# Swapped rows in the 2x2 products of a SwiGLU FFN, joined banks in another order, and modulation steps held in a chunk's last pair

## The chip, the cores and the metric

One core of one Trainium2 chip. The metric is the device time of one execution in microseconds; a kernel's time is the median of its runs. The engines are named as in the profile: PE (TensorE, matmuls), DVE (VectorE), ACT (ScalarE), POOL (GpSimd), SP (SyncE, which issues the DMAs here).

## The reference

A trunk of two layers on 640 tokens (128 context, 512 latent) with a width of 1024. Each layer is a SwiGLU FFN, a token mixer of three head groups, and a second FFN; each of the three is modulated by (shift, scale, gate) and closed by a layer norm. The change touches the FFNs alone:

```
def _modulation(cond, w, b):
    return (jax.nn.silu(cond) @ w + b).reshape(cond.shape[0], N_MOD, D_MODEL)

def _ffn_half(x, mod, slot, w1, w3, w2, g, b):
    h = _modulate(x, mod[:, 3 * slot], mod[:, 3 * slot + 1])
    f = (jax.nn.silu(h @ w1) * (h @ w3)) @ w2
    return _residual_post_norm(x, f, mod[:, 3 * slot + 2], FFN_RES, g, b)
```

d_ff is 2816, which is 22 tiles of 128. There are four FFNs in all.

## The kernel before

**Numbers in two parts.** Every matrix operand is held as a high and a low part (hh and hl, wh and wl, gh and gl): a cast on ACT makes the high part, a subtraction the low one. A product takes three matmuls for each step of the contraction: high by high, low by high, high by low. Weights come by DMA into a raw ring of two tiles (wr, L243), are cast by ACT into a ring of six (wh, L299), and the low part wl is a subtraction at L306 on DVE, or on POOL for two of the seven blocks of a pair (s2 and s4). A raw tile is free for the next DMA when its wl is done.

**Chunks.** The 22 tiles of d_ff are taken in chunks of 4, 3, 3, 4, 4 and 4 (ffn, the loop over CHUNKS). The first three tiles of an FFN are made plainly; all others are made by the class Pair: the j-th tile of w1 stands as the top row of a 2x2 block matrix, that of w3 as the bottom row, and the product with the 2x2 blocks of the modulated input (half of the contraction by half, LO and HI, of the 640 columns) is made by seven block products in place of eight. The sums of weight blocks are formed on POOL (L259). Each block product is `prod`: 12 matmuls of 128x320 (L847). The order of the seven on PE is p1, p2, p4, p6, p7, p5, p3.

**What follows a product.** `prod` ends with slot(), which runs the functions that were put off, and then puts off its own; what a function returns runs one slot later. So the work behind a product is emitted behind the next product, and a chain of steps takes one slot each. m is the running sum (pm), g the gate operand (gf), sl the silu operand. C11 = p1+p2 (LO half of the top row), C12 = m+p3 (its HI half), C21 = m-p4 and C22 = m+p5 (the bottom row), with m+p6 and m+p7 on the way. Before, the top row is w1, so silu acts on C11 (c11, L863) and C12 (c12, L877), and g is C21 and C22; gate1 (through L858) and gate2 (L881) multiply, hi (L886) casts gh, lo (L891) makes gl. For the last pair of a chunk the LO half is split on its own (half, L477 and L478) and hi and lo take the HI half; for the other pairs they take all 640 columns.

**The end of a chunk.** After the last pair two tiles of w2 (d0 and d1) are begun with all tiles of the contraction but the last; then the last one is added, half 0 of d0 and d1, half 1 of both (L485), which needs the last pair's gh and gl; tiles d2 to d7 follow, each with its residual on DVE (L610). The weight tiles d0 to d4 are converted ahead, while the last pair runs.

**Banks.** PSUM is held as two joined tiles of two banks (dbl) and four single banks (bank). Before, p4 and p5 share a joined tile; p1, p2, p6, p7 and p3 take single banks. The w2 tiles take joined ones too.

**Modulation on DVE.** In three of the four FFNs part of the next modulation vectors is made on DVE as rows of multiplications with a sum (L460, in the profile scr<-wv,cb; L463 closes one). `mods` adds to a credit at each call and takes as many steps as there is credit. It is called after p2, after p6 and after p5 in every pair, and after each w2 tile.

**The order.** Each engine works through its instructions in the order in which the program emits them; there is no planner.

Of the kernel before, what the change touches and what calls it, by code (L numbers as in the profile page):

```python
# [7 lines left out]
F32 = mybir.dt.float32  # L8
# [10 lines left out]
T = 640  # L19
# [86 lines left out]
def trunk_kernel(tc, I, O):  # L106
# [3 lines left out]
    with ExitStack() as es:  # L110
# [25 lines left out]
        def u(p, n, dt=F32, cols=T, nm="u"):  # L136
            return p.tile([P, cols], dt, tag=nm, name=n)
# [3 lines left out]
        def uid():  # L141
            cnt[0] += 1
            return cnt[0]
# [202 lines left out]
        def start(g):  # L346

            next(g)
            tasks.append(g)
# [480 lines left out]
        class Pair:  # L830


            def __init__(self, h, tb, last):
                self.last = last
                self.b11, self.b21, self.b22 = ([[a[:, c] for a in h[k]] for k in ks]
                                                for ks, c in ((range(4), slice(0, HN)), (range(4, 8), slice(0, HN)),
                                                              (range(4, 8), slice(HN, T))))
                self.t1, self.t2, self.t3, self.t4 = (Quarter(tb, i) for i in range(4))
                self.m, self.sl = u(pe_, f"pm{uid()}"), None

            def out(self):
                self.gh, self.gl = u(pe_, f"gh{uid()}", F32R), u(pe_, f"gl{uid()}", F32R)
                return self.gh, self.gl

            def mms(self, out, w, b, k):
                for i, (a, c) in enumerate(((0, 0), (0, 1), (1, 0))):
                    PE.matmul(out[:, :HN], w[a][:, k, :], b[k][c], start=k == 0 and i == 0, stop=k == 3 and i == 2)  # L847

            def prod(self, out, b, post=None, w=None):
                w = w or ws.get()  # L850
                for k in range(4):
                    self.mms(out, w, b, k)
                slot()
                if post:
                    later.append(post)
# [1 line left out]
            def op(self, o, a, b, f):  # L857
                V.tensor_tensor(out=o, in0=a, in1=b[:, :HN], op=f)  # L858

            def c11(self, p2):  # L860
                self.sl = u(pe_, f"sl{uid()}")
                self.op(self.sl[:, LO], self.m[:, LO], p2, ALU.add)
                return lambda: S.activation(self.sl[:, LO], self.sl[:, LO], AF.Silu) and None  # L863

            def gate1(self):
                self.op(self.g[:, LO], self.g[:, LO], self.sl, ALU.mult)
                return self.half if self.last else None

            def half(self):
                split(self.gh[:, LO], self.gl[:, LO], self.g[:, LO])  # L870

            def c12(self, p3):
                self.op(self.sl[:, HI], self.m[:, LO], p3, ALU.add)
                return self.silu2

            def silu2(self):
                S.activation(self.sl[:, HI], self.sl[:, HI], AF.Silu)  # L877
                return self.gate2

            def gate2(self):  # L880
                V.tensor_tensor(out=self.g[:, HI], in0=self.g[:, HI], in1=self.sl[:, HI], op=ALU.mult)  # L881
                return self.hi

            def hi(self):
                c = HI if self.last else slice(0, T)
                S.copy(self.gh[:, c], self.g[:, c])  # L886
                return self.lo

            def lo(self):
                c = HI if self.last else slice(0, T)  # L890
                V.tensor_tensor(out=self.gl[:, c], in0=self.g[:, c], in1=self.gh[:, c].bitcast(F32), op=ALU.subtract)  # L891

            def start(self):
                p1, p2 = bank("p1"), bank("p2")
                self.prod(p1, self.b11, lambda: S.copy(self.m[:, LO], p1[:, :HN]) and None)
                self.prod(p2, self.b21, lambda: self.c11(p2))

            def run(self, mods, begun=False):
                m, op = self.m, self.op
                if not begun:  # L900
                    self.start()
                mods(0)
                p45 = dbl("p4")
                p4, p5 = p45[:, 0, :], p45[:, 1, :]
                self.prod(p4, self.t4)
                p6 = bank("p6")
                self.prod(p6, self.t2, lambda: op(m[:, LO], m[:, LO], p6, ALU.add))
                mods(1)
                p7 = bank("p7")

                def u3():
                    op(m[:, HI], m[:, LO], p7, ALU.add)
                    self.g = u(pe_, f"gf{uid()}")
                    op(self.g[:, LO], m[:, HI], p4, ALU.subtract)
                    return self.gate1
                self.prod(p7, self.t3, u3)

                def u4():
                    op(self.g[:, HI], m[:, HI], p5, ALU.add)
                    op(m[:, LO], m[:, LO], p5, ALU.add)  # L920
                self.prod(p5, self.t1, u4)
                mods(2)
                p3 = bank("p3")
                self.prod(p3, self.b22, lambda: self.c12(p3))

            def run_first(self, mods, other, ts):

                m, op = self.m, self.op
                self.start()
                mods(0)  # L930
                other.start()
                p3 = bank("p3")
                self.prod(p3, self.b22, None, ws.get(4))
                w22 = ws.get(0)
                p45, p6, p7 = dbl("p4"), bank("p6"), bank("p7")
                p4, p5 = p45[:, 0, :], p45[:, 1, :]
                wq = [ws.get(0), ws.get(0), ws.get(2), w22]
                for k in range(4):
                    for o, w, b in zip((p5, p7, p6, p4), wq, (self.t1, self.t3, self.t2, self.t4)):
                        self.mms(o, w, b, k)  # L940
                    mods(k)
                    next(ts, 0)
                slot()

                def post():
                    self.g = u(pe_, f"gf{uid()}")
                    op(m[:, LO], m[:, LO], p6, ALU.add)
                    op(m[:, HI], m[:, LO], p7, ALU.add)
                    op(self.g[:, LO], m[:, HI], p4, ALU.subtract)
                    op(self.g[:, HI], m[:, HI], p5, ALU.add)  # L950
                    op(m[:, LO], m[:, LO], p5, ALU.add)
                    later.append(self.gate1)
                    return self.c12(p3)
                later.append(post)

        LO, HI = slice(0, HN), slice(HN, T)

# [58 lines left out]
        def ffn(l, f, h, first, nmod, nvec, norm, scale_x, tb, ts):  # L1016
# [5 lines left out]
            ws.convert(ws.n + 2)  # L1022
            ws.lows()

            def mods(when=None):
                if vec[0]:
                    credit[0] += (4 * nvec + 4) / 95 * (1 if when is None else 1)
                    while credit[0] >= 1:
                        credit[0] -= 1
                        next(vec[0], None)  # L1030
                if when is not None and when != 1 and not (f == 0 and ci == 0):
                    return
                if n_left[0]:
# [978 lines left out]
        for l in range(DEPTH):  # L2012
            for f in range(2):
                for j0, j1 in CHUNKS:
                    for j in range(j0, j1):
                        tw = [I["w13"][l, f, j, :, wi] for wi in range(2)]
                        if j < NC:
                            for wi in range(2):
                                ws.tile(tw[wi], (KD, P), "m" if 2 * j + wi == NOPEN else None)
                            continue  # L2020
                        r = ws.pair(*tw)
                        for nm in BLOCKS:
                            ws.block(nm, r)
# [176 lines left out]
```

## Time and profile before

| | |
|---|---|
| Median of three runs | 2698.13 us |
| Lowest and highest | 2695.59, 2703.82 us |
| The profiled execution | 2705.26 us |
| Its span | 2703.3 us |
| PE busy | 2555.0 us, 95% |
| DVE busy | 2072.3 us, 77% |
| ACT busy | 1175.9 us, 43% |
| POOL busy | 1244.0 us, 46% |
| PE waiting for DVE L858 (banks) | 16.8 us, 8 times |
| PE waiting for ACT L886 (gh) | 11.7 us, 13 times |

The span is what the profiler saw of the one execution that was profiled. Shares are of that span. A wait is an engine's idle time before an instruction, put down to the releaser that came last. Busy time of DVE, ACT and POOL counts for the end only where PE waits for it.

### The profile page before, as it was taken

How to read it: one execution, taken by the hardware profiler on the slowest of the kernel's cores; microseconds unless marked ns; L12 is line 12 of the kernel's file. 1: busy time of each engine (PE TensorE's matmuls, PEld its weight loads, DVE VectorE, ACT ScalarE, POOL GpSimd, SP SyncE). 2: the span in 40 equal slices, each digit the busy share in tenths (PEclk: the TensorE clock that was granted, in tenths of full speed). 3: DMA queues.
4: the chain of work that ended last, by engine and by line, in shares of the span. 5: the costliest groups of instructions: out<-in, count | busy, mean ns of one | idle time of the engine just before them, and what ended most of it. 6: DMA issues, size and time to landing. Idle time of an engine off the chain costs nothing. (4 is left out here: it accounts for less than half of the span.)

```text
span 2703.3 us, 49877 instructions
## 1 busy us (share of the span) xinstructions
PE 2555.0 (95%) x18662; PEld 2453.0 (91%) x18662; DVE 2072.3 (77%) x3759; ACT 1175.9 (43%) x2596; POOL 1244.0 (46%) x973
## 2 busy tenths in 40 slices
PE   7999999899999999999989999998998999999997
PEld 6999999888778999999989999998887798999997
DVE  6599889856764879988987998898476558777776
ACT  5233333545575533333353333334545745334333
POOL 2345445522444554544555454454233456435545
PEclk9999999999999999999989999998999999999998
DMA  7333332354344223333222333323543331222222
GB/s 273 116 98 101 111 97 83 117 152 136 91 130 156 71 96 100 103 101 109 68 83 84 112 103 101 110 87 108 158 134 98 103 114 40 82 82 87 79 86 71
DMA packets 130545, 285.89 MB, mean 106 GB/s; under 512 B 16832, under 2 KB 34560, under 8 KB 129664
## 3 DMA queue, kind: packets, MB, share of 16 engines
q1 hardware_dynamic: 130304, 282.70, 33.2%
q8 instruction: 148, 2.42, 0.4%
q14 instruction: 93, 0.76, 0.1%
HBM read 254.95 MB, written 8.81 MB: 98 GB/s over the span
## 5 line engine op out<-in xcount | busy, mean ns | idle before, releaser
L306 DVE TENSOR_TENSOR wl<-wr,wh 128x512 fp32r<-128x512 f32 (+1 forms) x524 | 518.3, 1003 | 74.1 <-ACT wh L299 72.5
L299 ACT CAST wh<-wr 128x512 fp32r<-128x512 f32 (+1 forms) x570 | 333.3, 607 | 479.4 <-DMA wr<-in_w 296.9
L485 PE MATMUL o<-gh,wh 128*128 128x256 f32 (+1 forms) x1408 | 439.5, 312 | 19.4 <-ACT gh L886 11.7
L485 PE MATMUL o<-gl,wh 128*128 128x256 f32 (+1 forms) x1408 | 439.0, 312 | 1.8 <-DVE gl L478 0.3
L485 PE MATMUL o<-gh,wl 128*128 128x256 f32 (+1 forms) x1408 | 436.7, 310 | 0.0
L847 PE MATMUL p<-hh,wh 128*128 128x320 f32 x1216 | 378.4, 311 | 16.8 <-DVE pm L858 16.8
L847 PE MATMUL p<-hl,wh 128*128 128x320 f32 x1216 | 378.2, 311 | 6.2 <-DVE hl L1010 6.2
L847 PE MATMUL p<-hh,wl 128*128 128x320 f32 x1216 | 378.1, 311 | 0.0
L259 POOL TENSOR_TENSOR ws<-wr 128x512 f32<-128x512 f32 x76 | 111.5, 1468 | 545.8 <-DMA wr<-in_w 482.8
L299 ACT CAST wh<-ws 128x512 fp32r<-128x512 f32 x304 | 185.9, 621 | 361.6 <-PE p L847 153.4
L306 POOL TENSOR_TENSOR wl<-ws,wh 128x512 fp32r<-128x512 f32 x152 | 241.3, 1591 | 193.6 <-ACT wh L299 193.1
L610 DVE SCALAR_TENSOR_TENSOR x<-o,gat,x 128x128 f32<-128x128 f32 (+2 forms) x404 | 192.9, 524 | 139.6 <-PE o L485 136.6
L485 PEld LDWEIGHTS o<-gh,wh 128*128 128x128 f32 x1408 | 267.8, 190 | 23.0 <-ACT gh L886 14.5
L485 PEld LDWEIGHTS o<-gl,wh 128*128 128x128 f32 x1408 | 268.1, 190 | 6.7 <-DVE gl L891 4.8
L485 PEld LDWEIGHTS o<-gh,wl 128*128 128x128 f32 x1408 | 267.9, 190 | 0.0
L847 PEld LDWEIGHTS p<-hh,wh 128*128 128x128 f32 x1216 | 229.9, 189 | 19.0 <-issue 18.9
L847 PEld LDWEIGHTS p<-hl,wh 128*128 128x128 f32 x1216 | 230.0, 189 | 7.4 <-DVE hl L1010 7.4
L847 PEld LDWEIGHTS p<-hh,wl 128*128 128x128 f32 x1216 | 230.0, 189 | 0.3 <-DVE wl L306 0.3
L460 DVE SCALAR_TENSOR_TENSOR scr<-wv,cb 128x512 f32<-128x512 f32 x192 | 181.2, 944 | 0.0
L259 POOL TENSOR_TENSOR ws<-wr,wr 128x512 f32<-128x512 f32 x76 | 130.2, 1713 | 0.0
L259 POOL TENSOR_TENSOR ws<-wr,ws 128x512 f32<-128x512 f32 x76 | 129.9, 1709 | 0.0
L259 POOL TENSOR_TENSOR ws<-ws,wr 128x512 f32<-128x512 f32 x76 | 119.1, 1567 | 6.0
(434 smaller groups left out, 6633.9 us busy)
## 6 DMA issues: line engine op xcount, KB each, us to landing
wr<-in_w SPq DMA_DIRECT2D x176, 512.0 KB, 4.2
wm<-in_wmod SPq DMA_DIRECT2D x192, 256.0 KB, 3.9
wr<-in_w SPq DMA_DIRECT2D x128, 256.0 KB, 2.7
wv<-in_wmt SPq DMA_DIRECT2D x96, 256.0 KB, 4.0
wr<-in_w SPq DMA_DIRECT2D x64, 192.0 KB, 2.4
wr<-in_wint SPq DMA_DIRECT2D x24, 512.0 KB, 4.2
wr<-in_wo SPq DMA_DIRECT2D x16, 512.0 KB, 3.8
xd<-x SPq DMA_DIRECT2D x16, 320.0 KB, 5.1
```

Of the source, the lines that this page charges most:

```text
L259: G.tensor_tensor(out=o, in0=x0, in1=x1, op=op)
L299: S.copy(hl[0], src[:, c0:c1])
L306: eng.tensor_tensor(out=t2, in0=src, in1=t.bitcast(F32), op=ALU.subtract)
L460: V.scalar_tensor_tensor(out=scr, in0=w[2 * i + hf], scalar=1.0, in1=cb[:, 2 * st + hf, :], op0=ALU.mult, op1=ALU.mult, accum_out=a[:, 2 * ...
L485: PE.matmul(out[:, :cn], whl[a][:, k, :], b[:, c0:c0 + cn], start=k == 0 and i == 0, stop=k == n - 1 and i == 2)
L610: V.scalar_tensor_tensor(out=c, in0=src, scalar=gat[:, d, s:s + 1], in1=c, op0=ALU.mult, op1=ALU.add)
L847: PE.matmul(out[:, :HN], w[a][:, k, :], b[k][c], start=k == 0 and i == 0, stop=k == 3 and i == 2)
```

## The change

Three things are changed, and the number of instructions stays the same on each engine.

1. **The rows are swapped.** The pair is built as (w3, w1) in place of (w1, w3). The top row is now w3 and the bottom row w1. So silu acts on C21 and C22 (from p4, p5, p6, p7), and the gate operand g is C11 and C12 (from p2 and p3). After p3 there stand: the addition into g, gate HI, gh, gl. The steps move between slots accordingly: silu LO in the slot after p3, gate LO, silu HI, c12 and gate HI in the slot after the next p1, the cast of gh after the next p2, gl after the next p4.
2. **The banks.** p6 and p7 now share a joined tile, as p4 and p5 do. p1, p2 and p3 take single banks.
3. **Modulation.** In the last pair of a chunk the calls of mods after p6 and after p5 add to the credit and take no step; the credit is spent in the calls that follow.

The rest of the diff drops functions that nothing calls.

```
-            def gate1(self):
-                self.op(self.g[:, LO], self.g[:, LO], self.sl, ALU.mult)
-                return self.half if self.last else None
...
+            def gate(self, c):
+                V.tensor_tensor(out=self.g[:, c], in0=self.g[:, c], in1=self.sl[:, c], op=ALU.mult)
+
+            def split(self, c):
+
                 S.copy(self.gh[:, c], self.g[:, c])
-                return self.lo
...
+                def lo():
+                    V.tensor_tensor(out=self.gl[:, c], in0=self.g[:, c], in1=self.gh[:, c].bitcast(F32), op=ALU.subtract)
+                return lo
+
+            def run(self, mods):
+                m, op = self.m, self.op
                 p1, p2 = bank("p1"), bank("p2")
...
+                def c11():
+                    self.g = u(pe_, f"gf{uid()}")
+                    op(self.g[:, LO], m[:, LO], p2, ALU.add)
+                self.prod(p1, self.b11, lambda: S.copy(m[:, LO], p1[:, :HN]) and None)
+                self.prod(p2, self.b21, c11)
                 mods(0)
-                p45 = dbl("p4")
-                p4, p5 = p45[:, 0, :], p45[:, 1, :]
+                p67, p45 = dbl("p6"), dbl("p4")
+                p4, p5, p6, p7 = (p[:, i, :] for p in (p45, p67) for i in range(2))
                 self.prod(p4, self.t4)
-                p6 = bank("p6")
                 self.prod(p6, self.t2, lambda: op(m[:, LO], m[:, LO], p6, ALU.add))
-                mods(1)
-                p7 = bank("p7")
...
+                mods(1, self.last)
+
+                def c21():
+                    self.sl = u(pe_, f"sl{uid()}")
                     op(m[:, HI], m[:, LO], p7, ALU.add)
...
+                    op(self.sl[:, LO], m[:, HI], p4, ALU.subtract)
+
+                    def silu():
+                        S.activation(self.sl[:, LO], self.sl[:, LO], AF.Silu)
+                        return gate1
+                    return silu
+
+                def gate1():
+                    self.gate(LO)
+                    return (lambda: self.split(LO)) if self.last else None
+                self.prod(p7, self.t3, c21)
+
+                def c22():
+                    op(self.sl[:, HI], m[:, HI], p5, ALU.add)
+                    op(m[:, LO], m[:, LO], p5, ALU.add)
+                    return lambda: S.activation(self.sl[:, HI], self.sl[:, HI], AF.Silu) and None
+                self.prod(p5, self.t1, c22)
+                mods(2, self.last)
                 p3 = bank("p3")
...
+                def c12():
+                    op(self.g[:, HI], m[:, LO], p3, ALU.add)
+                    self.gate(HI)
+                    return lambda: self.split(HI if self.last else slice(0, T))
+                self.prod(p3, self.b22, c12)
...
-            def mods(when=None):
+            def mods(when=None, hold=False):
                 if vec[0]:
                     credit[0] += (4 * nvec + 4) / 95 * (1 if when is None else 1)
-                    while credit[0] >= 1:
+                    while credit[0] >= 1 and not hold:
                         credit[0] -= 1
                         next(vec[0], None)
...
-                        r = ws.pair(*tw)
+                        r = ws.pair(*tw[::-1])
```

DVE in the last pair of the fourth chunk, second FFN of layer 0, before: wl_13730 and wl_13752 are the low parts of w2's d0 and d1, gl_13531 that of the pair before, wl_13773 that of d2.

```order
L460 SCALAR_TENSOR_TENSOR scr_11797,va_13723<-wv_13301,cb_11114 128x512
L881 TENSOR_TENSOR gf_13659<-gf_13659,sl_13590 128x320
L858 TENSOR_TENSOR sl_13745<-pm_13682,p_13686 128x320
L306 TENSOR_TENSOR wl_13730<-wr_13639,wh_13729 128x512
L306 TENSOR_TENSOR wl_13752<-wr_13641,wh_13751 128x512
L891 TENSOR_TENSOR gl_13531<-gf_13659,gh_13530 128x640
L858 TENSOR_TENSOR pm_13682<-pm_13682,p_13747 128x320
L306 TENSOR_TENSOR wl_13773<-wr_13749,wh_13772 128x512
```

DVE at the same place after: wl_13704 and wl_13725 are d0 and d1, gl_13502 is the pair before's, wl_13743 is d2.

```order
L865 TENSOR_TENSOR gl_13502<-gf_13565,gh_13501 128x640
L855 TENSOR_TENSOR gf_13719<-pm_13652,p_13656 128x320
L306 TENSOR_TENSOR wl_13704<-wr_13609,wh_13703 128x512
L306 TENSOR_TENSOR wl_13725<-wr_13611,wh_13724 128x512
L855 TENSOR_TENSOR pm_13652<-pm_13652,p_13700 128x320
L306 TENSOR_TENSOR wl_13743<-wr_13722,wh_13742 128x512
```

The low part of the pair before moved from behind the two wl's to ahead of both.

ACT in the same last pair before: wh_13772, wh_13792 and wh_13815 are the casts of d2, d3 and d4; sl_13745, gh_13683 belong to the last pair, sl_13590 and gh_13530 to the one before.

```order
L877 ACTIVATE sl_13590<-sl_13590 128x320
L895 COPY pm_13682<-p_13685 128x320
L299 CAST wh_13729<-wr_13639 128x512
L299 CAST wh_13751<-wr_13641 128x512
L886 CAST gh_13530<-gf_13659 128x640
L863 ACTIVATE sl_13745<-sl_13745 128x320
L299 CAST wh_13772<-wr_13749 128x512
L299 CAST wh_13792<-wr_13770 128x512
L299 CAST wh_13815<-wr_13790 128x512
L477 CAST gh_13683<-gf_13808 128x320
L877 ACTIVATE sl_13745<-sl_13745 128x320
L886 CAST gh_13683<-gf_13808 128x320
```

ACT at the same place after: wh_13742, wh_13761 and wh_13783 are d2, d3 and d4; sl_13776 and gh_13653 belong to the last pair, sl_13628 and gh_13501 to the one before; wh_13678 is the block s4.

```order
L902 ACTIVATE sl_13628<-sl_13628 128x320
L299 CAST wh_13678<-ws_13604 128x512
L862 CAST gh_13501<-gf_13565 128x640
L875 COPY pm_13652<-p_13655 128x320
L299 CAST wh_13703<-wr_13609 128x512
L299 CAST wh_13724<-wr_13611 128x512
L299 CAST wh_13742<-wr_13722 128x512
L299 CAST wh_13761<-wr_13740 128x512
L299 CAST wh_13783<-wr_13759 128x512
L890 ACTIVATE sl_13776<-sl_13776 128x320
L902 ACTIVATE sl_13776<-sl_13776 128x320
L862 CAST gh_13653<-gf_13719 128x320 x2
```

Both silus of the last pair now stand behind the cast of d4; before, the first stood ahead of d2's. The cast of s4 stands behind the second silu of the pair before.

DVE from the last products to the residuals, before:

```order
L460 SCALAR_TENSOR_TENSOR scr_11797,va_13723<-wv_13301,cb_11114 128x512
L306 TENSOR_TENSOR wl_13793<-wr_13770,wh_13792 128x512
L858 TENSOR_TENSOR gf_13808<-gf_13808,sl_13745 128x320
L858 TENSOR_TENSOR gf_13808<-pm_13682,p_13727 128x320
L858 TENSOR_TENSOR pm_13682<-pm_13682,p_13727 128x320
L478 TENSOR_TENSOR gl_13684<-gf_13808,gh_13683 128x320
L858 TENSOR_TENSOR sl_13745<-pm_13682,p_13811 128x320
L881 TENSOR_TENSOR gf_13808<-gf_13808,sl_13745 128x320
L891 TENSOR_TENSOR gl_13684<-gf_13808,gh_13683 128x320
L306 TENSOR_TENSOR wl_13816<-wr_13790,wh_13815 128x512
```

DVE there after:

```order
L306 TENSOR_TENSOR wl_13762<-wr_13740,wh_13761 128x512
L855 TENSOR_TENSOR sl_13776<-pm_13652,p_13701 128x320
L855 TENSOR_TENSOR pm_13652<-pm_13652,p_13701 128x320
L858 TENSOR_TENSOR gf_13719<-gf_13719,sl_13776 128x320
L855 TENSOR_TENSOR gf_13719<-pm_13652,p_13779 128x320
L858 TENSOR_TENSOR gf_13719<-gf_13719,sl_13776 128x320
L865 TENSOR_TENSOR gl_13654<-gf_13719,gh_13653 128x320 x2
L306 TENSOR_TENSOR wl_13784<-wr_13759,wh_13783 128x512
```

The modulation step (L460) ahead of d3's wl is gone from here, the first multiplication stands behind the additions of p5, and both halves of gl come last.

## Rows read from the trace of the kernel before

**Rows 1.** The page, section 1: busy time, share of the span, instructions.

```profile
PE 2555.0 (95%) x18662; PEld 2453.0 (91%) x18662; DVE 2072.3 (77%) x3759; ACT 1175.9 (43%) x2596; POOL 1244.0 (46%) x973
```

**Rows 2.** Waits of PE: engine, line, releaser: total us, times, longest.

```profile
PE p L847 <- DVE pm L858: 16.8, 8, 3.5
...
PE o L485 <- ACT gh L886: 11.7, 13, 1.1
```

**Rows 3.** Timeline of PE, example chunk: start us, us, line, operation, [idle before <-releaser].

```profile
1161.89 0.39 PE L847 MATMUL p<-hh,wh 128*128 128x320 f32 x1 [1.94 <-DVE pm L858]
...
1178.41 0.28 PE L485 MATMUL o<-gl,wh 128*128 128x256 f32 x1
1178.53 0.28 PE L485 MATMUL o<-gh,wl 128*128 128x256 f32 x1
1179.87 0.44 PE L485 MATMUL o<-gh,wh 128*128 128x384 f32 x1 [1.06 <-ACT gh L886]
1180.40 0.44 PE L485 MATMUL o<-gl,wh 128*128 128x384 f32 x1
```

**Rows 4.** Timeline of ACT at the end of the same chunk.

```profile
1176.39 0.62 ACT L299 CAST wh<-wr 128x512 fp32r<-128x512 f32 x1 [2.77 <-DMA wr<-in_w]
1176.92 0.45 ACT L477 CAST gh<-gf 128x320 fp32r<-128x320 f32 x1
1178.33 0.47 ACT L877 ACTIVATE sl<-sl 128x320 f32<-128x320 f32 x1 [0.96 <-DVE sl L858]
1179.36 0.46 ACT L886 CAST gh<-gf 128x320 fp32r<-128x320 f32 x1 [0.56 <-DVE gf L881]
```

**Rows 5.** Timeline of DVE in the same chunk, third and last pair.

```profile
1154.55 1.57 DVE L881 TENSOR_TENSOR gf<-gf,sl 128x320 f32<-128x320 f32 x1
...
1159.45 1.90 DVE L891 TENSOR_TENSOR gl<-gf,gh 128x640 fp32r<-128x640 f32 x1
1161.27 0.47 DVE L858 TENSOR_TENSOR pm<-pm,p 128x320 f32<-128x320 f32 x1
...
1168.08 0.48 DVE L881 TENSOR_TENSOR gf<-gf,sl 128x320 f32<-128x320 f32 x1
...
1168.89 1.28 DVE L306 TENSOR_TENSOR wl<-wr,wh 128x512 fp32r<-128x512 f32 x2
1170.09 0.82 DVE L891 TENSOR_TENSOR gl<-gf,gh 128x640 fp32r<-128x640 f32 x1
1170.83 0.48 DVE L858 TENSOR_TENSOR pm<-pm,p 128x320 f32<-128x320 f32 x1
1172.98 0.69 DVE L306 TENSOR_TENSOR wl<-wr,wh 128x512 fp32r<-128x512 f32 x1 [1.67 <-ACT wh L299]
1173.59 0.48 DVE L858 TENSOR_TENSOR pm<-pm,p 128x320 f32<-128x320 f32 x1
1174.17 0.49 DVE L858 TENSOR_TENSOR gf<-pm,p 128x320 f32<-128x320 f32 x1
...
1178.84 0.49 DVE L881 TENSOR_TENSOR gf<-gf,sl 128x320 f32<-128x320 f32 x1 [0.54 <-ACT sl L877]
```

**Rows 6.** Timeline of SP's queue in the same chunk: when DMAs were issued.

```profile
1169.60 12.30 SPq L243 DMA_DIRECT2D wr<-in_w  x6
```

**Rows 7.** Timeline of POOL in the same chunk.

```profile
1158.94 3.54 POOL L306 TENSOR_TENSOR wl<-ws,wh 128x512 fp32r<-128x512 f32 x2
```

**Rows 8.** Timeline of PE at the end of the fifth chunk, first FFN.

```profile
396.46 0.34 PE L485 MATMUL o<-gh,wh 128*128 128x384 f32 x1
396.63 0.34 PE L485 MATMUL o<-gl,wh 128*128 128x384 f32 x1
```

**Rows 9.** Timeline of DVE there.

```profile
393.71 0.49 DVE L891 TENSOR_TENSOR gl<-gf,gh 128x320 fp32r<-128x320 f32 x1 [0.53 <-ACT gh L886]
```

**Rows 10.** Windows: stretch, its length, busy us of PE, PEld, DVE, ACT, POOL, PEclk, DMA share, GB/s.

```profile
1103.40:1106.80 3.40, 3.40 (x15) 3.40 (x15) 3.40 (x10) 1.02 (x2) 0.00 (x0) 0.50 0.59 180
...
376.30:383.20 6.90, 6.10 (x23) 6.13 (x24) 6.76 (x16) 1.30 (x3) 0.00 (x0) 0.51 0.34 107
```

More of the change, by code (lines that the diff above doesn't have):

```diff
@@ L838, in __init__ @@
                 self.t1, self.t2, self.t3, self.t4 = (Quarter(tb, i) for i in range(4))
-                self.m, self.sl = u(pe_, f"pm{uid()}"), None
+                self.m = u(pe_, f"pm{uid()}")
             def out(self):
@@ L843, in out, with prod @@
                 return self.gh, self.gl
[L845 to L850, printed above, removed]
+            def prod(self, out, b, post=None):
+                w = ws.get()
                 for k in range(4):
-                    self.mms(out, w, b, k)
+                    for i, (a, c) in enumerate(((0, 0), (0, 1), (1, 0))):
+                        PE.matmul(out[:, :HN], w[a][:, k, :], b[k][c], start=k == 0 and i == 0, stop=k == 3 and i == 2)
                 slot()
@@ L858, in op @@
                 V.tensor_tensor(out=o, in0=a, in1=b[:, :HN], op=f)
[L860 to L863, printed above, removed]
-            def gate1(self):
-                self.op(self.g[:, LO], self.g[:, LO], self.sl, ALU.mult)
-                return self.half if self.last else None
-            def half(self):
-                split(self.gh[:, LO], self.gl[:, LO], self.g[:, LO])
@@ L872, in c12 @@
[L872 to L885, printed above, removed]
-                S.copy(self.gh[:, c], self.g[:, c])
-                return self.lo
@@ L889, in lo @@
[L889 to L893, printed above, removed]
-                p1, p2 = bank("p1"), bank("p2")
[L895 to L901, printed above, removed]
+            def gate(self, c):
+                V.tensor_tensor(out=self.g[:, c], in0=self.g[:, c], in1=self.sl[:, c], op=ALU.mult)
@@ L902, in run @@
                 mods(0)
-                p45 = dbl("p4")
-                p4, p5 = p45[:, 0, :], p45[:, 1, :]
+                p67, p45 = dbl("p6"), dbl("p4")
+                p4, p5, p6, p7 = (p[:, i, :] for p in (p45, p67) for i in range(2))
                 self.prod(p4, self.t4)
-                p6 = bank("p6")
                 self.prod(p6, self.t2, lambda: op(m[:, LO], m[:, LO], p6, ALU.add))
-                mods(1)
-                p7 = bank("p7")
-                def u3():
+                mods(1, self.last)
@@ L912, in u3 @@
+                def c21():
+                    self.sl = u(pe_, f"sl{uid()}")
                     op(m[:, HI], m[:, LO], p7, ALU.add)
[L913 to L919, printed above, removed]
+                    op(self.sl[:, LO], m[:, HI], p4, ALU.subtract)
[3 more added lines that the diff above has]
+                    return silu
@@ L920, in u4 @@
+                def gate1():
[4 more added lines that the diff above has]
+                    op(self.sl[:, HI], m[:, HI], p5, ALU.add)
                     op(m[:, LO], m[:, LO], p5, ALU.add)
-                self.prod(p5, self.t1, u4)
-                mods(2)
+                    return lambda: S.activation(self.sl[:, HI], self.sl[:, HI], AF.Silu) and None
@@ L923, in run @@
+                self.prod(p5, self.t1, c22)
+                mods(2, self.last)
                 p3 = bank("p3")
[L924 to L954, printed above, removed]
```

## The prediction

> **What bounds the kernel now.** The page comes first: TensorE (PE) is busy 95% of a span of 2703.3 us [rows 1]. Only its waits can be won, so the second view is PE's waits by releaser: 16.8 us for VectorE (DVE) line L858, eight times, at most 3.5, and 11.7 us for the ScalarE (ACT) cast of gh at L886, 13 times, at most 1.1 [rows 2]. They are the two places that the change touches: a product that finds no free bank, and the end of a chunk, where the w2 rows need the last pair's gh and gl.
>
> The third view is PE's timeline in one chunk, the fourth chunk of layer 0's second FFN [rows 3]. The bank wait: the second product of the last pair starts 1.94 us late, since DVE has not yet read p6 of the pair before. The chunk end: the last tile's half 1 waits 1.06 us for gh, and its second matmul comes 0.53 us later where 0.17 is the pitch of these when nothing waits [rows 8]; together 1.4 us.
>
> The fourth step is to ask what ended that wait last, on ACT and DVE. ACT's cast of w2 tile d4 begins at 1176.39 after 2.77 us of idle for its DMA, and behind it, in order, stand gh's first half, the second silu and gh's second half [rows 4]. The second half-1 matmul runs 4.01 us after the start of the d4 cast. I followed this in all 15 later chunks of the three FFNs that make modulation on DVE: in 14 the matmul comes 3.9 (chunks of three pairs) to 4.1 us after that cast, and the cast always ends an idle time for its DMA. One chunk, the fifth of the first FFN, has no wait there.
>
> The d4 DMA in turn goes back to DVE: the raw ring holds two tiles, so d2's DMA is issued when DVE has finished wl of d0 [rows 5, 6] (1168.89 to 1169.5, issue at 1169.60), and d4's after wl of d2 (1172.98). So **the end of a waiting chunk is set by the moment DVE reaches wl d0**, some 7.5 us ahead of the d4 cast. PE's bank wait in the same chunk is slack that this chain swallows: a product that starts sooner only waits longer at the end.
>
> **The bank order.** Before, p2 waits for m+p6 of the pair before and p6 for m+p7; after, p4 waits for m+p7 and p6 for m+p5. Each is five product starts behind what it waits for, so the allowance is the same: five starts of 12 matmuls at 0.15 us, less the product itself and a hop, about 6.8 us from the end of a product to the end of its DVE reading. In the third pair of a four-pair chunk DVE is late at all three by nearly the same time (the 1.94 us in [rows 3] is that excess). gate1, of the size of the 0.48 us multiplication in [rows 5] (pitch 0.4), no longer stands ahead of m+p5, so that one gains 0.4. I expect waits of 1.5 to 2.1 us to stay, two products later, and to be worth nothing in the 14 chunks.
>
> **The swapped rows.** silu now acts on C21 and C22, which are ready before p3. Behind p3 remain add, gate, gh, gl: one silu and one hop between engines fewer. Yet both silus of the last pair now stand behind the d4 cast on ACT, where before the first stood ahead of it. With the pitches of [rows 4, 5] from the start of the cast: silu LO +0.53 (1176.92), gate LO a hop of 0.51 later (1178.33 to 1178.84) +1.04, c12 +1.45, gate HI, which reads what c12 has just written (0.58 apart, as 1173.59 and 1174.17), +2.03, gh HI +2.55 (hop 0.52), gl LO +2.44, gl HI +3.04. PE's first matmul with gl LO follows at +2.99 (hop 0.55, 1179.85 to 1180.40); five pitches of 0.12 (1178.41 to 1178.53 in [rows 3]) and one of 0.17 bring the second half-1 matmul to +3.76, and gl HI, at +3.04 with a hop of 0.55, is in time. Against 4.01 that is **0.25 us sooner**. The silu saved after p3 is mostly lost to the silu that must wait for d4.
>
> **The earlier gl.** The gl of the pair before (640 columns, 0.74 of pitch, 1170.09 to 1170.83) stood behind wl d0 and wl d1 and now stands ahead of both [rows 5]. This moves wl d0, the d2 DMA and the whole chain: +0.74. It could be +1.0 if gl also waits 0.3 for gh's cast, and less if DVE gets there sooner. For that there is a reason: GpSimd (POOL) runs its two subtractions of the last pair at 1158.94 for 3.54 us [rows 7], and under them gl takes 1.90 us, where alone it takes 0.82. L881 takes 1.57 us under POOL work and 0.48 alone [rows 5]. After, the second subtraction waits for an ACT cast that stands behind silu HI, 0.7 to 1.1 us later, so its end falls beside additions that read a bank and take 0.47 under POOL work (1161.27) and 0.48 without. I estimate 0 to 0.6 us saved by this. So wl d0 shifts by 0.1 to 1.0 us; I take 0.45, near the middle, as neither end has a row of its own. The change per chunk end is 0.45 - 0.25 = +0.2, times 14 = **+2.8 us** (bounds -0.15 x 14 = -2.1 and +0.75 x 14 = +10.5).
>
> The Trainium skill, "SBUF — State Buffer", section "Who interferes with whom", has VectorE and GpSimd share a port pair as an exclusive lock, taken for a whole instruction by VectorE operations with two SBUF inputs. The trace agrees in kind: gate and gl, with both inputs in SBUF, stretch by 1.1 us, and those with one input in a bank do not. By that lock a gl that now meets a POOL operation at its start would wait for all of it, and the chunk end would come later by up to that one operation.
>
> **No modulation in the last pair.** The multiplications held are one or two per last pair, moved into the rows; I count each as long as the subtraction of the same 128x512 shape at 1172.98, 0.69 us [rows 5]. They stood after wl d2, with d4 still under way: DVE idles there later for ACT all the same (0.54 us ahead of L881 [rows 5]), so taking them out brings 0 at the end of the chunk. In the rows PE is full and DVE has time, cost 0; before the norm of each FFN some 1.4 more steps drain, 1.4 x 0.69 = 1.0 us, three times, of which I take none, since PE has the last rows' matmuls to do meanwhile; if that cover is gone the price is 3 us. No DMA is added. The weight tiles of the modulation are fetched on SP's queue as steps are taken, so they are issued later, beside the rows.
>
> **The free chunk.** The fifth chunk of the first FFN has the longest bank wait, 3.5 us [rows 2], and PE's second half-1 matmul at 396.63 comes 2.4 us after what the last gl (start 393.71, hop 0.55) allows [rows 8, 9]. Here a shorter bank wait would count, up to those 2.4. I take -1.0 (bounds 0 and -2.4).
>
> **The clock.** After a wait PE's granted clock can fall to the lower of its two levels, 1.2 GHz: 0.50 for 3.4 us from 1103.40, after a chunk end; 0.51 over 376.3 to 383.2, around that 3.5 us bank wait [rows 10]. A 3.4 us stretch at half clock costs 1.7 us. Of the 14 chunk ends with a wait one was followed by such a stretch, of seven waits near 2 us two. After the change the idle at the chunk end lies in one stretch ahead of gh LO and gl LO (about 0.7 + 0.8 us, plus the shift), so I take one more fall, **+1.7 us** (bounds -3.4 to +13.6, below).
>
> **Sum.** +2.8 - 1.0 + 1.7 = +3.5 us. The profiled execution took 2705.26 us, 2.0 more than its span and 7 above the median of the runs, as one of the slower of them; the sum moves it to 2708.8. On the median of 2698.13 it gives **2702 us**.
>
> **Rival 1, faster.** POOL's later subtraction frees DVE for more than I take. Under POOL work the chunk shown loses 1.09 us on the L881 of 1154.55 and 1.08 on gl at 1159.45, 2.2 together [rows 5]. If all of that goes, wl d0 comes 2.2 - 0.74 = 1.4 us sooner in the eight waiting four-pair chunks, as much as their end wait: -1.4 x 8 = -11.2. The six chunks of three pairs gain 0.25 to 1 each (-3.5), the free chunk 2.4. Total -17: **2681 us**. For it: every one of these operations has two inputs in SBUF. Against it: POOL's work is only moved, and s4 now runs beside wl s1, scr and gl of the next stretch, which have two SBUF inputs as well. Chance 0.25.
>
> **Rival 2, slower.** The clock falls after most of the longer chunk ends: eight four-pair chunks at 1.7 us = +13.6, with +2.8 and -2.4 gives +14: **2712 us**. It decides once the one idle stretch at the chunk end is as long as the bank waits that brought falls, some 2 us, which is the case where wl d0 shifts by 0.7 or more. For it: the bank wait now lies one or two products nearer to the chunk end's. Against it: most waits of 2 us brought no fall. The same sign at a lower price (+10.5 - 1 = 2708) comes if wl d0 shifts the full 1.0. Chance 0.25 together.
> The Trainium skill, "TensorE: Matmul & The Clock Gate", section "HAM oscillation — how this bites in real kernels", tells of waits in a loop that throttle TensorE anew each time round. The trace agrees for single waits (0.50 and 0.51 above), not for a fall at every chunk.
>
> **Rival 3, the change is swallowed.** The end of a chunk stays on its DMA chain with the shift and the shorter tail equal (0.25 each), and nothing else counts: 2698, within the forecast's own range. Chance 0.1.
>
> **How the numbers follow.** Forecast 0.4 (own range 2692 to 2710), rival 1 0.25, rival 2 0.25, rival 3 0.1. About 0.3%, 8 us, is what a measurement of this kernel can tell from no change: faster means below 2690, slower above 2706. Faster has rival 1 but its small outcomes, and a little of the forecast: 0.25. Slower has rival 2 and the upper end of the forecast: 0.26. The rest is 0.49. The range that leaves out 2 in 10 runs from 2684 (most of rival 1) to 2714 (rival 2).
>
> **What would show it.** In the profile of the changed kernel the four-pair chunks keep a bank wait of about 2 us, now at the third or fourth product of the last pair; the d4 cast still ends an idle time for its DMA; the second half-1 matmul comes 3.7 to 3.8 us after it instead of 4.0; wl d0 follows a 640-column gl. Rival 1 shows as gl and wl of normal length there and a last pair without waits; rival 2 as more stretches at 0.50. The forecast is wrong if the d4 cast no longer waits for its DMA, or if PE waits for a wl of POOL's that the later subtraction delays.

## The result

The changed kernel takes 2710.41 us against 2696.47 us in the same comparison: a ratio of **1.0054, 95% interval 1.0043 to 1.0066**, some 14 us slower. The time lies in the predicted range (2684 to 2714), but the likeliest case, no measurable difference at 2702 us, did not come. The profiled execution after has a span of 2703.4 us, where that of before had 2703.3: the one of before was one of its slower executions, the one after one of its faster, so the two spans side by side say nothing. What compares are the stretches of the trace that repeat in each chunk.

The waits of PE after, by releaser (total us, times, longest), to be held against [rows 2]:

```profile
PE o L485 <- DVE pm L855: 29.1, 15, 2.8
...
PE p L849 <- DVE wl L306: 3.2, 7, 1.2
PE o L485 <- DVE gl L865: 3.2, 6, 0.5
...
PE p L849 <- DVE pm L855: 2.7, 6, 0.5
...
PE o L485 <- ACT gh L862: 0.7, 3, 0.4
```

The product's wait for a bank fell from 16.8 to 2.7 us, and the wait for gh from 11.7 to 0.7. New are waits for a low part, 3.2 us for wl and 3.2 for gl. In place of what fell stands one that no line of before has: 29.1 us in which a w2 matmul waits for m+p7 (pm, L855), once in each of the 15 later chunks of the three FFNs with modulation on DVE. PE's timeline of the example chunk, which answers to [rows 3], shows where it is; then ACT's and DVE's, which answer to [rows 4, 5]:

```profile
1173.70 0.31 PE L849 MATMUL p<-hh,wl 128*128 128x320 f32 x1
1176.83 0.36 PE L485 MATMUL o<-gh,wh 128*128 128x256 f32 x1 [2.83 <-DVE pm L855]
...
1182.88 0.34 PE L485 MATMUL o<-gh,wh 128*128 128x384 f32 x1
1183.06 0.34 PE L485 MATMUL o<-gl,wh 128*128 128x384 f32 x1
```

```profile
1174.95 1.34 ACT L299 CAST wh<-wr 128x512 fp32r<-128x512 f32 x2 [3.72 <-DMA wr<-in_w]
1178.92 0.62 ACT L299 CAST wh<-wr 128x512 fp32r<-128x512 f32 x1 [2.63 <-DMA wr<-in_w]
1179.45 0.47 ACT L890 ACTIVATE sl<-sl 128x320 f32<-128x320 f32 x1
1179.82 0.45 ACT L902 ACTIVATE sl<-sl 128x320 f32<-128x320 f32 x1
1180.48 0.46 ACT L862 CAST gh<-gf 128x320 fp32r<-128x320 f32 x1 [0.20 <-DVE gf L858]
1181.47 0.46 ACT L862 CAST gh<-gf 128x320 fp32r<-128x320 f32 x1 [0.53 <-DVE gf L858]
```

```profile
1170.37 0.82 DVE L865 TENSOR_TENSOR gl<-gf,gh 128x640 fp32r<-128x640 f32 x1
1171.11 0.47 DVE L855 TENSOR_TENSOR gf<-pm,p 128x320 f32<-128x320 f32 x1
1171.51 1.28 DVE L306 TENSOR_TENSOR wl<-wr,wh 128x512 fp32r<-128x512 f32 x2
1172.71 0.47 DVE L855 TENSOR_TENSOR pm<-pm,p 128x320 f32<-128x320 f32 x1
1175.60 0.69 DVE L306 TENSOR_TENSOR wl<-wr,wh 128x512 fp32r<-128x512 f32 x1 [2.41 <-ACT wh L299]
1176.21 0.48 DVE L855 TENSOR_TENSOR pm<-pm,p 128x320 f32<-128x320 f32 x1
...
1179.95 0.49 DVE L858 TENSOR_TENSOR gf<-gf,sl 128x320 f32<-128x320 f32 x1 [1.27 <-ACT sl L890]
1180.36 0.48 DVE L855 TENSOR_TENSOR gf<-pm,p 128x320 f32<-128x320 f32 x1
1180.94 0.49 DVE L858 TENSOR_TENSOR gf<-gf,sl 128x320 f32<-128x320 f32 x1
1181.35 1.10 DVE L865 TENSOR_TENSOR gl<-gf,gh 128x320 fp32r<-128x320 f32 x2
```

The last product is issued at 1173.70 and the first w2 matmul only at 1176.83. Its tile is a joined one, and with p6 and p7 in a joined tile both of them belong to the last pair. m+p7, the reading that frees it (1176.21), stands on DVE behind the low part of d2 (1175.60), and that waits for ACT's cast (1174.95), so for d2's DMA. At this chunk's end there is no wait any more: the second half-1 matmul runs at 1183.06, 4.14 us after the start of the d4 cast.

### The profile page after: what moved, and what is told of

Same layout as the page of the kernel before. It is cut to its first block, busy times and chain, and to the rows that moved or that the text cites. A ratio compares the mean times of both kernels' runs of the same rounds, so it can differ in the third digit from the quotient of the medians.

```text
span 2703.4 us, 49869 instructions
## 1 busy us (share of the span) xinstructions
PE 2546.8 (94%) x18662; PEld 2441.3 (90%) x18662; DVE 2044.8 (76%) x3759; ACT 1173.3 (43%) x2596; POOL 1248.5 (46%) x973
## 5 line engine op out<-in xcount | busy, mean ns | idle before, releaser
L306 DVE TENSOR_TENSOR wl<-wr,wh 128x512 fp32r<-128x512 f32 (+1 forms) x524 | 521.0, 1012 | 91.1 <-ACT wh L299 90.7
L485 PE MATMUL o<-gh,wh 128*128 128x256 f32 (+1 forms) x1408 | 443.3, 315 | 38.2 <-DVE pm L855 29.1
L306 POOL TENSOR_TENSOR wl<-ws,wh 128x512 fp32r<-128x512 f32 x152 | 244.5, 1612 | 228.9 <-ACT wh L299 224.7
L460 DVE SCALAR_TENSOR_TENSOR scr<-wv,cb 128x512 f32<-128x512 f32 x192 | 170.9, 890 | 0.5
L855 DVE TENSOR_TENSOR pm<-pm,p 128x320 f32<-128x320 f32 x228 | 109.1, 478 | 40.3 <-PE p L849 40.3
L858 DVE TENSOR_TENSOR gf<-gf,sl 128x320 f32<-128x320 f32 x152 | 103.3, 679 | 37.4 <-ACT sl L890 29.1
```

The lines of the kernel that those rows point to most:

```text
L306: eng.tensor_tensor(out=t2, in0=src, in1=t.bitcast(F32), op=ALU.subtract)
L460: V.scalar_tensor_tensor(out=scr, in0=w[2 * i + hf], scalar=1.0, in1=cb[:, 2 * st + hf, :], op0=ALU.mult, op1=ALU.mult, accum_out=a[:, 2 * ...
L485: PE.matmul(out[:, :cn], whl[a][:, k, :], b[:, c0:c0 + cn], start=k == 0 and i == 0, stop=k == n - 1 and i == 2)
L858: V.tensor_tensor(out=self.g[:, c], in0=self.g[:, c], in1=self.sl[:, c], op=ALU.mult)
```

## The experiments

The change has three parts, and a fourth thing came with it (gl's new place). All ratios below are to the kernel before, run on the same chip at the same time.

**The new bank wait.** Two kernels take it away in different ways. The first begins the w2 tile in single banks first and the joined one second:

```
-                    p = dbl("o") if d == 0 else [bank("o"), bank("o")]
+                    p = [bank("o"), bank("o")] if d == 0 else dbl("o")
```

> The changed kernel, but of the two w2 tiles begun behind the last pair the first takes the two single banks and the second the joined tile. Theory A (the change costs because the joined tile that p6 and p7 now hold makes the first w2 matmul wait for m+p7, and that stands on DVE behind the low part of d2, so behind d2's DMA): the first tile's matmuls (1.8 us in chunks of three pairs, 2.6 us in those of four) run under the wait; of the 31.5 us that PE loses ahead of the first w2 matmul in the 15 chunks under 8 stay, the second half-1 matmul comes 3.75 us after the start of the d4 cast in the four-pair chunks in place of 3.96 to 4.13, the idle is cut in two and fewer chunk ends are followed by half clock: 2699 to 2705 us. Theory B (it costs because gl stands ahead of the low part of d0, so all of d2, d3, d4 come later): the end of the chunk stays on the d4 cast, 2708 to 2711 us.

1.0031 (1.0012 to 1.0050), at the upper end of what theory A had; the interval overlaps that of the change, so the gain itself is not clear of noise. The wait is not simply gone, another stands in its place, where theory A had left under 8 us; PE's waits:

```profile
PE o L485 <- ACT gh L862: 17.1, 15, 1.8
...
PE o L485 <- DVE gl L865: 8.0, 16, 0.6
```

29.1 us for the bank became 25 us for gh and gl at the end of the same chunks. The second kernel has the banks of before and the other two parts:

```
-                p67, p45 = dbl("p6"), dbl("p4")
-                p4, p5, p6, p7 = (p[:, i, :] for p in (p45, p67) for i in range(2))
+                p45 = dbl("p4")
+                p4, p5 = p45[:, 0, :], p45[:, 1, :]
...
+                p6 = bank("p6")
...
+                p7 = bank("p7")
```

> The changed kernel with the banks of before (p4 and p5 in a joined tile, p6 and p7 in single banks); rows swapped and modulation held as in the change. Theory A: no wait of the first w2 matmul (0.15 us as before), bank waits of 2 us back at the second or fourth product of the last pair, where the chunk's end swallows them: 2697 to 2704 us. Theory B: 2708 to 2711 us.

1.0053 (1.0034 to 1.0072): nothing is won by it. The expectations were made against 2696.5 us for before, so theory A had at most 1.003 here. It falls as the whole account. Why the second is not as fast as the first stays open; their intervals overlap. The clock can have hidden it: PE's granted clock averages 0.979 over the first kernel's runs and 0.977 over the second's, which I estimate, from 0.002 of 2700, at some 5 us, and the two ratios lie 6 us apart. Against A speaks also the other direction, the banks alone on the kernel before (p67 as in the change, nothing else):

> The kernel before, with p6 and p7 in a joined tile and nothing else of the change. Theory A: PE waits at the first w2 matmul for m+p7, 1 to 2 us in the four-pair chunks, of which the chunk's own end wait (1.4 us) hides most, so 2696 to 2703 us; if the bank alone is enough to make the loss it is 2706 or more. Theory B: no difference from before, 2693 to 2699 us.

0.9997 (0.9983 to 1.0011). PE waits there too for m+p7 at the first w2 matmul, and the time does not change: the chunk's own end wait shrinks by as much, from 11.7 to 4.1 us. (The products' waits for a bank grow from 16.8 to 19.4 us, and the granted clock averages 0.983 over these runs against 0.979 over those of before; that the clock gives back a small price is not excluded.)

```profile
PE o L485 <- DVE pm L858: 6.6, 10, 1.0
...
PE o L485 <- ACT gh L886: 4.1, 6, 0.8
```

**Holding the modulation.** The kernel before with that part alone:

```
-                mods(1)
+                mods(1, self.last)
...
-                mods(2)
+                mods(2, self.last)
...
-            def mods(when=None):
+            def mods(when=None, hold=False):
...
-                    while credit[0] >= 1:
+                    while credit[0] >= 1 and not hold:
```

> The kernel before, with the modulation steps of the last pair held and nothing else of the change. Theories A and B: no difference, 2693 to 2700 us. Theory C (the held steps crowd the w2 rows or the wait ahead of the norm): 2701 us or more, with waits of PE for DVE's residuals in the rows.

1.0028 (1.0013 to 1.0043). The part that I had priced at zero costs some 7 us by itself. It is not the clock: the granted clock averages 0.980 over these runs and 0.979 over those of before. The change without it:

> The changed kernel without the holding of modulation steps: rows swapped and banks as in the change. Theory C (the held steps land in the w2 rows, where DVE has as much to do per tile as PE in the chunks of three pairs, and delay the raw ring there): additive, ratio 1.0015 to 1.004; w2 rows of the three-pair chunks back to 15.8 us. If the loss of holding alone was particular to the old order: 1.005 to 1.006.

1.0012 (0.9999 to 1.0025), and with the banks of before as well, so that only the swapped rows are left:

> The swapped rows alone: banks of before, no holding. Theory C (holding is the main price) and the prediction's sum for the swap (about +0.2 us for each waiting chunk): 0.9995 to 1.002 of before. If the joined tile of p6 and p7 had a price of its own with the rows swapped, this is at least 0.001 below the 1.0012 of rows and banks without holding; if it had none, the two are equal within the intervals.

1.0011 (0.9997 to 1.0025). The kernels form a table (ratio to before):

| rows | banks | without holding | with holding |
|---|---|---|---|
| old | old | 1 | 1.0028 |
| old | joined p6, p7 | 0.9997 | not run |
| swapped | old | 1.0011 | 1.0053 |
| swapped | joined p6, p7 | 1.0012 | 1.0054 |

Down each column the banks make no difference. Holding costs 0.28% with the old rows and 0.42% with the swapped ones, whichever the banks; whether it costs more with the swapped rows is not clear of noise. What the rows cost, 0.11%, is less than can be told from zero.

**Where holding costs.** In the w2 rows of a chunk of three pairs. DVE's timeline at the second chunk of layer 0's second FFN, first of the changed kernel, then of the one without holding; both begin with the last pair's gl:

```profile
1042.75 1.10 DVE L865 TENSOR_TENSOR gl<-gf,gh 128x320 fp32r<-128x320 f32 x2
1043.77 1.02 DVE L306 TENSOR_TENSOR wl<-wr,wh 128x384 fp32r<-128x384 f32 x2
1044.71 1.01 DVE L610 SCALAR_TENSOR_TENSOR x<-o,gat,x 128x512 f32<-128x512 f32 x2
1045.63 0.68 DVE L460 SCALAR_TENSOR_TENSOR scr<-wv,cb 128x512 f32<-128x512 f32 x1
...
1046.36 0.69 DVE L460 SCALAR_TENSOR_TENSOR scr<-wv,cb 128x512 f32<-128x512 f32 x1
...
1046.98 1.13 DVE L610 SCALAR_TENSOR_TENSOR x<-o,gat,x 128x256 f32<-128x256 f32 x3
...
1048.76 0.56 DVE L306 TENSOR_TENSOR wl<-wr,wh 128x384 fp32r<-128x384 f32 x1
```

```profile
1036.96 1.10 DVE L865 TENSOR_TENSOR gl<-gf,gh 128x320 fp32r<-128x320 f32 x2
1037.98 1.02 DVE L306 TENSOR_TENSOR wl<-wr,wh 128x384 fp32r<-128x384 f32 x2
1038.92 2.05 DVE L610 SCALAR_TENSOR_TENSOR x<-o,gat,x 128x512 f32<-128x512 f32 x5
...
1041.63 0.56 DVE L306 TENSOR_TENSOR wl<-wr,wh 128x384 fp32r<-128x384 f32 x1
1042.10 1.01 DVE L610 SCALAR_TENSOR_TENSOR x<-o,gat,x 128x512 f32<-128x512 f32 x2
...
1044.71 1.01 DVE L610 SCALAR_TENSOR_TENSOR x<-o,gat,x 128x512 f32<-128x512 f32 x2 [0.53 <-PE o L485]
```

The two held multiplications (1045.63 and 1046.36) stand between the residuals of d0 and d1. The next low part comes 6.01 us after gl with them and 4.67 without. That low part frees a raw tile, and the DMA goes with it (6.60 against 5.25 us after gl):

```profile
1049.35 0.33 SPq L243 DMA_DIRECT2D wr<-in_w  x1
```

```profile
1042.21 0.33 SPq L243 DMA_DIRECT2D wr<-in_w  x1
```

Without holding DVE has caught up with PE two tiles later (the 0.53 us of idle at 1044.71); with it, DVE has no such idle in these rows, and enters the next chunk behind: the first addition of that chunk comes 24.3 us after gl in place of 23.2. The residuals of two tiles in a row stand 2.61 us apart there (1042.10 and 1044.71; the expectation quoted below says 2.3, which is too low), the time that PE takes for a tile. DVE has 0.5 us of low part, 0.9 of residual and 0.6 of multiplication to do for it, and more in the last tiles, where the low parts of the next pair's blocks take 0.6 to 1.8 us each: there is little room to catch up. Part of the price is paid at the end of the next chunk: wl d0 comes 0.4 to 1.2 us later there than without holding, and the first w2 matmul waits for m+p7. PE's waits from those rows to the end of that chunk's tiles, changed kernel and without holding:

```profile
PE o L485 <- DVE pm L855: 1.7, 1, 1.7
```

```profile
PE o L485 <- DVE pm L855: 0.4, 1, 0.4
```

In these two traces the six chunks of three pairs, each taken from the last w2 matmul of the chunk before to its own last, add up to 364.1 us with holding and 359.6 without, 4.5 more. The rest of the 11 us lies in the chunks behind them, where the two executions also had their falls of the clock at different places, so how it splits is not shown. With the old rows the place is the same: in the kernel that only holds, the products of the second three-pair chunk take 0.4 to 0.65 us longer than before.

A kernel that holds in the chunks of four pairs alone tests the place:

```
-                    while credit[0] >= 1 and not hold:
+                    while credit[0] >= 1 and not (hold and n == 4):
```

> The changed kernel, holding the modulation steps only in the chunks of four pairs. Theory C (holding costs because the held steps land in the w2 rows of the chunks of three pairs, where a tile takes PE 2.3 us and DVE has as much to do): nearly all of the holding's price is gone, ratio to before 1.000 to 1.003, with the second three-pair chunk and the four-pair chunk behind it as in the kernel without holding. If holding costs in every chunk alike (eight or nine of fifteen still hold): 1.003 to 1.005.

1.0017 (1.0005 to 1.0029): nine of the fifteen last pairs still hold, and of the 0.42% at most a small part is left. So it is the holding in the six chunks of three pairs that costs, and that it costs anything in the others, the ones ahead of the norm among them, is not shown.

**gl's place, the silu, and the mends together.** gl of the pair before, one slot later in the changed kernel:

```
-                    return lambda: self.split(HI if self.last else slice(0, T))
+                    return lambda: self.split(HI) if self.last else (lambda lo: lambda: lo)(self.split(slice(0, T)))
```

> The changed kernel, with gl of the pair before taken one slot later, so that it stands behind the low part of d0 instead of ahead of it. Theory B (the gl that was pulled ahead of d0 delays d2's DMA and all that follows it): wl d0 comes 0.5 to 0.8 us earlier in the last pair, the d4 cast and the wait of the first w2 matmul (which hangs on wl d2) come earlier by the same, 15 chunks: ratio to before 1.001 to 1.003 in place of 1.0054. Theory A (only the bank): the bank is still read late, 1.004 to 1.006. Theory D (DVE is simply behind by the same work whatever its order): 1.004 to 1.006 with wl d0 earlier but the matmul not.

1.0063 (1.0044 to 1.0082), where theory B had 1.001 to 1.003. wl d0 does come sooner (in the trace by 0.3 to 0.6 us in the fifth and sixth chunks), but the profile shows half clock at six of the nine four-pair chunk ends, where the changed kernel has three. Theory B is not borne out; the size of gl's place alone stays open behind the clock. The first silu of the last pair ahead of the d4 cast:

```
-                    return silu
+                    return silu() if self.last else silu
```

> The changed kernel, with the first silu of the last pair issued right behind the subtraction that makes its operand, so that on ACT it stands ahead of the cast of d4. The tail behind the d4 cast shortens: silu HI at +0.5, gate HI about +1.5, gh HI +2.0, gl HI +2.5 us in place of +3.04. Theory A: in the four-pair chunks the first w2 matmul's wait for its bank is what ends the chunk, so little is won there (0.3 us in chunks of three pairs): ratio 1.004 to 1.006. If instead the two silus behind d4 are what costs: 1.001 to 1.003.

1.0039 (1.0025 to 1.0053), which overlaps the change too. The tail is as short as expected (gl HI 2.3 to 2.4 us behind the d4 cast in place of 3.0), and as expected the four-pair chunks give most of it to the bank wait. All of it together, without holding:

> The changed kernel without holding, with the single banks for the first of the two w2 tiles, gl one slot later and the first silu ahead of the d4 cast. If the three causes are the whole loss: 0.993 to 0.999 of before, with waits of PE at the end of a chunk below those of before (gl HI 2.5 us after the d4 cast where before had 3.5). If something else of the swapped order costs, 1.000 or more.

**0.9965 (0.9950 to 0.9980)**, 2679.65 us against 2692.24: faster than both kernels. The waits that answer to those above:

```profile
PE o L485 <- DVE gl L865: 13.2, 14, 1.1
...
PE p L849 <- DVE pm L855: 2.8, 6, 0.5
...
PE o L485 <- ACT gh L862: 0.6, 2, 0.3
...
PE o L485 <- DVE pm L855: 0.4, 1, 0.4
```

And the same with gl where the change has it:

> The kernel with the mends but with gl of the pair before where the change has it, ahead of the low part of d0. Theory B: wl d0 0.5 us later in each of 15 chunks, 0.998 to 1.001 of before. If gl's place is worth nothing: 0.995 to 0.998, as with it.

0.9972 (0.9962 to 0.9982). The intervals overlap: once the bank wait and the holding are gone, gl's place is worth nothing that can be measured. With the silu in front of the d4 cast and the single banks first, the kernel is 0.4% below the same kernel without these two (0.9972 against 1.0012). So a kernel with swapped rows can be faster than before; that the rows are what makes it so is not shown, as the single banks first were not tried with the old rows.

One step further failed. It stops the conversion ahead at d3 in the last pair, so that d4's cast stands behind the gates:

```
-                w = ws.get()
+                w = ws.get(ahead)
...
-                self.prod(p3, self.b22, c12)
+                self.prod(p3, self.b22, c12, 4 if self.last else None)
```

> The kernel with all four mends (no holding, single banks for the first w2 tile, gl one slot later, first silu early), and in the last pair of a chunk the conversion ahead stops at d3, so that d4's cast stands behind the silus and gates on ACT. If the end of a chunk is set by the d4 DMA through ACT's order, as the traces of before and of all variants so far say, this takes the wait away: PE's idle at the chunk ends falls from some 1.3 us to under 0.5 in most chunks, 0.987 to 0.994 of before. If DVE's own lag sets it, 0.995 to 0.998 as without this step.

1.0131 (1.0115 to 1.0148), slower by 35 us. The chunk ends did get shorter (8.7 us of waits for gl in place of 13.2), and PE waited in the rows for DVE's residuals instead:

```profile
PE o L485 <- DVE x L610: 36.5, 18, 3.5
```

The reason is argued from the order and not shown: d5's DMA waits for the low part of d3 and d6's for that of d4, so the weights of the rows came later, and the residuals stand behind their low parts.

## Why the prediction was right in its range and wrong in its likeliest case

That the time lies in the range is luck as far as the mechanism goes: the upper end was made for falls of the clock, and what filled it is a term that I had put at zero.

**The step that failed** is the one on modulation: "In the rows PE is full and DVE has time, cost 0." I looked at the last pair, where the steps were taken away and DVE idles, and did not read the stretch into which they were moved. In the rows of the three-pair chunks DVE has 2.0 us and more to do per tile, PE 2.6, and DVE feeds the raw ring. The term measured +0.28% (7 us) alone and +0.42% (11 us) beside the swapped rows, which is nearly all of the 14 us. I had named a price for the lost cover (3 us) only at the norm, and it was not there.

**The chain from wl d0 over the d2 and d4 DMAs** held in its order: the d4 cast still ends an idle time for its DMA, in the example 2.63 us. **The tail behind it** came out to the hundredth on ACT and DVE: gate HI, gh HI and gl LO were worked out at +2.03, +2.55 and +2.44 us, and the trace has them at 1180.94, 1181.47 and 1181.35, +2.02, +2.55 and +2.43. On PE it held in the six three-pair chunks alone, where the second half-1 matmul follows the d4 cast by 3.73 to 3.77 us (3.76 worked out). In the nine four-pair chunks it follows by 3.9 to 4.1 us, and by more where the clock falls: there the tail no longer sets the end, PE does, which has started late for want of the bank. The 0.25 us that I took as gained at each end did not come there.

**The earlier gl** was taken as +0.45 us at wl d0. Without holding, wl d0 stands on average 0.3 us later than before in both sorts of chunk; with holding 0.5 to 0.7. The sum that I made for the swap alone, +2.8 us with bounds -2.1 and +10.5, stands beside a measured 1.0011 (0.9997 to 1.0025), -1 to +7 us.

**The banks.** I expected the bank waits of the last pair to stay at 1.5 to 2.1 us. They shrank to 0.5 us at most, with 3.2 us of waits for a low part (wl, L306) new beside them, and a wait that I had not seen took their place: w2's first tile is a joined one too. That the change of banks costs nothing that the time shows is the part I had right, that a wait ahead of the chunk's end is swallowed by it, only at another place. Rival 1's signs did show, gl at 1170.37 with its normal 0.82 us, the two wl behind it with 1.28, and next to no bank waits in the last pair; but its gain did not come, since wl d0 stands later, not sooner.

**The free chunk** lost its wait of 3.5 us and got one of 2.7 for m+p7. From the end of the tiles before to the end of its own it takes 81.6 us against 83.9. The half clock around the old wait has its part in that, so neither the -1.0 nor its bounds are tested.

**The clock.** I took one more fall at a chunk end. The trace of after has three of nine four-pair ends at the lower level; one of them, from the first w2 matmul of the fifth chunk of layer 0's second FFN:

```profile
1258.30:1260.30 2.00, 1.93 (x9) 1.96 (x10) 1.89 (x4) 0.00 (x0) 0.00 (x0) 0.50 0.46 131
1260.30:1263.70 3.40, 3.40 (x13) 3.40 (x13) 1.91 (x5) 2.42 (x6) 0.00 (x0) 0.50 0.30 77
1263.70:1266.50 2.80, 2.80 (x19) 2.80 (x18) 1.57 (x3) 0.36 (x1) 0.00 (x0) 0.85 0.22 45
```

This is PEclk 0.50 for 5.4 us and a little into the third stretch, at the end of an idle of 2.7 us. Rival 2 named this mechanism, falls at most of the longer chunk ends, and had 2712 us, near the measured time. It was not the cause: without holding, the same wait for m+p7 remains and three ends fall as well, at 1.0012; and the granted clock averages 0.979 over the runs of the changed kernel, as it does over those of before (0.979 to 0.980).

## What to carry to other kernels

A step that is moved has two places. Work taken out of a stretch where the engine idles anyway wins nothing, and it costs in full where the engine has as much to do per tile as the one it feeds; so read the busy share of the stretch that receives it, tile by tile, before pricing it at zero. When a buffer is widened, list all that draw from its pool, also behind the loop that is changed. And where several waits end one behind the other, taking one away shows the next, so judge by the time and not by the wait that went. Here the gains added up all the same: taken from the change one by one, holding, bank order and silu gave 0.42, 0.23 and 0.15% (the last two not clear of noise), 0.80 together, and all three at once 0.82.

## What the runs showed of the hardware

PE's clock at a chunk end is close to a lottery. With a wait of 1.9 to 2.8 us in front of the first w2 matmul, the granted clock fell to 0.50 at three of nine four-pair ends in the changed kernel, at six with gl later, and at none in the kernel that holds in four-pair chunks alone; each fall cost 1.4 to 2.8 us. Cutting the wait in two did not help: with the swapped rows alone six of the nine ends fell, at waits of 1.1 to 1.9 us for gh and then 0.5 for gl. In the kernel with all the mends, where one wait of at most 1.1 us for gl is left, none did. These are one execution of each kernel. Over all runs the clock averages 0.977 with the rows alone, 0.979 to 0.980 before and 0.983 with the banks alone.

DVE's operations with two inputs in SBUF stretch while POOL works: the multiplication of 0.48 us to 1.57 and gl of 0.82 to 1.90 [rows 5]. In all fourteen traces a 640-column gl that runs wholly under POOL's work takes 1.9 us in the median and 0.82 without it, while the additions with an input in a bank take 0.47 to 0.49 either way.
